# Instance norm on one core: the 32 stores move from ScalarE's queue to GpSimd's, with one packet for each DMA engine

## The chip, the cores and the metric

The kernel runs on one core of a Trainium2 chip. The core has five engines with their own instruction streams (TensorE or PE, VectorE or DVE, ScalarE or ACT, GpSimd or POOL, SyncE or SP) and 16 DMA engines that move data between HBM, the chip's main memory, and the on-chip memory (SBUF, 128 partitions). A DMA is issued by one of SP, ACT and POOL, each of which has a queue of its own on all 16 DMA engines.

The metric is the device time in microseconds (us), lower is better: 627.08 us for the kernel before, the median of 3 runs from 626.85 to 627.26. Beside it stands one profiled execution, whose trace gives the times of single instructions and DMA packets.

## The reference

Each channel of `x` (4 batches, 8 groups, 16 channels: 512 channels of 256 x 256 float32) is normalised by its own mean and variance and multiplied by its gamma. 134.2 MB go in and 134.2 MB come out.

```python
def reference(x, gamma):          # x: (4, 8, 16, 256, 256), gamma: (8, 16)
    mu = x.mean(axis=(3, 4), keepdims=True)
    var = ((x - mu) ** 2).mean(axis=(3, 4), keepdims=True)
    x_norm = (x - mu) / np.sqrt(var + 1e-5)
    out = x_norm * gamma[None, :, :, None, None]
    return out.astype(np.float32)
```

## The kernel before

The data is cut into 32 units (`U`), each of 16 channels. A channel is spread over 8 partitions (`S`), so that a unit is a tile of 128 partitions x 8192 float32 (32 KB in each partition, 4.19 MB in all). Six such tiles (`slots`, `AHEAD` = 6) lie in SBUF and are used in rotation: unit u lives in slot u mod 6, is normalised in place and stored from there. A slot can be loaded anew once its store has landed.

The order of each engine's instructions is that of the program text (`manual_schedule`); the semaphores between engines and for the DMAs are put in by the framework.

Start (L53 to L94): DVE clears a small tile `touch`, which GpSimd stores over a part of the output that is later overwritten (L54); GpSimd loads gamma into one row, `g_row` (L55). Then the first six loads are issued (L56 and L57, through `load` at L47 and L48): units 1 and 3 by ScalarE, units 0, 2, 4 and 5 by SP. DVE has 60 no-operations (L59 and L60). GpSimd builds the averaging matrix `navg` (L67 to L72), which holds -1/HW where row and column belong to the same channel. DVE copies `g_row` into `g_rep` (L83), TensorE spreads it over the partitions (L88), DVE copies the result into `g_col` (L94).

Then for each unit u (L105 to L136):

- L107, DVE: sum of each partition's row, into `st`
- L108, ACT: sum of the squares of the same row, into `st`
- L116, PE: `navg` times `st`, which gives minus the mean and minus the mean square of each channel, on all of its partitions
- L117, DVE: minus the variance; L121, ACT: its root; L125 and L127, DVE: reciprocal, times gamma
- L130, DVE: (x - mean) times scale over the whole tile, in place
- L134, ACT: the store of the tile, which waits for L130
- L136, SP: the load of unit u + 6 into the same slot, which waits until this store has landed

The next unit's Square (L108) stands behind this unit's store in ScalarE's stream. SP has nothing but loads in its stream, and GpSimd nothing at all after the start.

Of the kernel before, what the change touches and what calls it, by code (L numbers as in the profile page):

```python
# [1 line left out]

# [4 lines left out]

F32 = mybir.dt.float32
U8 = mybir.dt.uint8
ALU = mybir.AluOpType  # L10
ACTF = mybir.ActivationFunctionType
AX = mybir.AxisListType


@with_exitstack
def kernel(
    ctx: ExitStack,
    tc: tile.TileContext,
    x: bass.AP,
    gamma: bass.AP,  # L20
    out: bass.AP,
):
    nc = tc.nc
    B, G, C, H, W = x.shape
    P = nc.NUM_PARTITIONS
    HW = H * W
    n_ch = B * G * C
    S = 8
    K = P // S
    F = HW // S  # L30
    U = n_ch // K
    NG = (G * C) // K
    AHEAD = 6
    assert HW % S == 0 and (G * C) % K == 0

    xv = x.rearrange("b g c h w -> (b g c h w)").rearrange("(u p f) -> u p f", p=P, f=F)
    ov = out.rearrange("b g c h w -> (b g c h w)").rearrange("(u p f) -> u p f", p=P, f=F)
    gv = gamma.rearrange("g c -> (g c)")

    data = ctx.enter_context(tc.tile_pool(name="data", bufs=1))  # L40
    singles = ctx.enter_context(tc.tile_pool(name="singles", bufs=1))
    psum = ctx.enter_context(tc.tile_pool(name="psum", bufs=4, space=bass.MemoryType.PSUM))
    ctx.enter_context(tc.manual_schedule())

    slots = [data.tile([P, F], F32, name=f"xt{i}") for i in range(AHEAD)]

    def load(u, queue):  # L47
        queue.dma_start(out=slots[u % AHEAD][:], in_=xv[u])  # L48


    g_row = singles.tile([1, G * C], F32, name="g_row")
    touch = singles.tile([16, 128], F32, name="touch")
    nc.vector.memset(touch[:], 0.0)  # L53
    nc.gpsimd.dma_start(out=ov[0][0::S, 0:128], in_=touch[:])  # L54
    nc.gpsimd.dma_start(out=g_row[:], in_=gv[None, :])  # L55
    for u in range(AHEAD):  # L56
        load(u, nc.scalar if u in (1, 3) else nc.sync)  # L57

    for _ in range(60):  # L59
        nc.vector.nop()  # L60

    eps_t = singles.tile([P, 1], F32, name="eps_t")
    nc.gpsimd.memset(eps_t[:], 1e-5)
    one = singles.tile([1, 1], F32, name="one")
    nc.gpsimd.memset(one[:], 1.0)
    navg = singles.tile([P, K, S], F32, name="navg")
    nc.gpsimd.memset(navg[:], -1.0 / HW)  # L67
    nc.gpsimd.affine_select(  # L68
        out=navg[:], in_=navg[:], pattern=[[-S, K], [0, S]], compare_op=ALU.is_ge,
        fill=0.0, base=0, channel_multiplier=1,  # L70
    )
    nc.gpsimd.affine_select(  # L72
        out=navg[:], in_=navg[:], pattern=[[S, K], [0, S]], compare_op=ALU.is_ge,
        fill=0.0, base=S - 1, channel_multiplier=-1,
    )
    navg_w = navg[:].rearrange("p k s -> p (k s)")
    root_eps = singles.tile([P, 1], F32, name="root_eps")
    nc.scalar.activation(out=root_eps[:], in_=eps_t[:], func=ACTF.Sqrt)  # L78
    g_rep = singles.tile([1, NG, K, S], F32, name="g_rep")
    g_ps = psum.tile([P, NG], F32, name="g_ps", bufs=1)  # L80
    g_col = singles.tile([P, NG], F32, name="g_col")

    nc.vector.tensor_copy(  # L83
        out=g_rep[:],
        in_=g_row[:].rearrange("o (n k) -> o n k", n=NG).unsqueeze(3).to_broadcast([1, NG, K, S]),
    )
    for n in range(NG):
        nc.tensor.matmul(  # L88
            out=g_ps[:, n : n + 1],
            lhsT=g_rep[:, n].rearrange("o k s -> o (k s)"),  # L90
            rhs=one[:],
            start=True, stop=True,
        )
    nc.vector.tensor_copy(out=g_col[:], in_=g_ps[:])  # L94

    junk = singles.tile([P, F], U8, name="junk")

    st = singles.tile([P, U, 2], F32, name="st")
    nvar = singles.tile([P, U], F32, name="nvar")
    std = singles.tile([P, U], F32, name="std")  # L100
    rstd = singles.tile([P, U], F32, name="rstd")
    scale = singles.tile([P, U], F32, name="scale")

    squares = []
    for u in range(U):  # L105
        t = slots[u % AHEAD]
        nc.vector.reduce_sum(out=st[:, u, 0:1], in_=t[:], axis=AX.X)  # L107
        square = nc.scalar.activation(  # L108
            out=junk[:], in_=t[:], func=ACTF.Square, accum_out=st[:, u, 1:2],
        )  # L110
        if u:

            tc.declare_no_dep(square.ins, squares[-1].ins, reason="junk, ordered by the root between")
        squares.append(square)
        ps = psum.tile([P, 2], F32, name="ps")
        nc.tensor.matmul(out=ps[:], lhsT=navg_w, rhs=st[:, u], start=True, stop=True)  # L116
        nc.vector.tensor_scalar(  # L117
            out=nvar[:, u : u + 1], in0=ps[:, 0:1], scalar1=ps[:, 0:1],
            scalar2=ps[:, 1:2], op0=ALU.mult, op1=ALU.add,
        )  # L120
        nc.scalar.activation(  # L121
            out=std[:, u : u + 1], in_=nvar[:, u : u + 1], func=ACTF.Sqrt,
            bias=eps_t[:], scale=-1.0,
        )
        nc.vector.reciprocal(out=rstd[:, u : u + 1], in_=std[:, u : u + 1])  # L125
        g = u % NG
        nc.vector.tensor_mul(  # L127
            out=scale[:, u : u + 1], in0=rstd[:, u : u + 1], in1=g_col[:, g : g + 1],
        )
        nc.vector.tensor_scalar(  # L130
            out=t[:], in0=t[:], scalar1=ps[:, 0:1], scalar2=scale[:, u : u + 1],
            op0=ALU.add, op1=ALU.mult,
        )
        nc.scalar.dma_start(out=ov[u], in_=t[:])  # L134
        if u + AHEAD < U:
            load(u + AHEAD, nc.sync)  # L136


# [1 line left out]
_INS = ['x', 'gamma']  # L140
_OUTS = [((4, 8, 16, 256, 256), 'float32')]


# [23 lines left out]
```

## Time and profile before

| | |
|---|---|
| median of 3 runs | 627.08 us (626.85 to 627.26) |
| span of the profiled execution | 625.8 us |
| moved by DMA | 268.46 MB, mean 429 GB/s over the span |
| DVE busy | 443.4 us (71%) |
| ACT busy | 238.8 us (38%) |
| PE busy | 21.4 us (3%) |
| POOL busy | 2.4 us |
| L107, reduce, DVE | 32 x 8684 ns |
| L130, scale, DVE | 32 x 4550 ns |
| L108, square, ACT | 32 x 7030 ns |
| load 31 has landed, L107 of unit 31 starts | at 586.12 us |
| store 31 is issued | at 601.17 us |

The span goes from the first to the last instruction of the program in the profiled execution; the runs' time is that of the whole execution on the device. Busy times of different engines overlap. A DMA's issue is a short instruction on the engine that issues it; the transfer runs by itself afterwards, and the profile gives its time to landing, from the issue until the completion semaphore. Queue numbers stand for the issuer: 1 is SP's, 10 is ScalarE's, 0 is GpSimd's.

### The profile page before, as it was taken

How to read it: one execution, taken by the hardware profiler on the slowest of the kernel's cores; microseconds unless marked ns; L12 is line 12 of the kernel's file. 1: busy time of each engine (PE TensorE's matmuls, PEld its weight loads, DVE VectorE, ACT ScalarE, POOL GpSimd, SP SyncE). 2: the span in 40 equal slices, each digit the busy share in tenths (PEclk: the TensorE clock that was granted, in tenths of full speed). 3: DMA queues.
4: the chain of work that ended last, by engine and by line, in shares of the span. 5: the costliest groups of instructions: out<-in, count | busy, mean ns of one | idle time of the engine just before them, and what ended most of it. 6: DMA issues, size and time to landing. Idle time of an engine off the chain costs nothing.

```text
span 625.8 us, 631 instructions
## 1 busy us (share of the span) xinstructions
PE 21.4 (3%) x80; PEld 19.5 (3%) x80; DVE 443.4 (71%) x163; ACT 238.8 (38%) x98; POOL 2.4 (0%) x11
## 2 busy tenths in 40 slices
PE   0200000000000000000000000000000000000000
PEld 0200000000000000000000000000000000000000
DVE  0588999999776687766776667867668676686730
ACT  0444444444443244432344423444224442244400
POOL 1000000000000000000000000000000000000000
DMA  8999999999999999999999999999999999999998
GB/s 369 436 415 429 429 436 436 436 436 434 424 434 434 434 436 434 431 429 434 436 436 436 436 431 427 431 436 431 436 434 434 429 434 436 436 436 436 429 425 354
DMA packets 9282, 268.46 MB, mean 429 GB/s; under 512 B 1072, under 2 KB 1088, under 8 KB 1088
## 3 DMA queue, kind: packets, MB, share of 16 engines
q10 hardware_dynamic: 4896, 142.61, 52.9%
q1 hardware_dynamic: 4320, 125.83, 46.7%
q0 software_dynamic: 64, 0.01, 0.0%
q14 instruction: 2, 0.02, 0.0%
HBM read 134.22 MB, written 134.23 MB: 429 GB/s over the span
## 4 chain that ended last, share of the span: by engine, by line
another core or an unknown queue 61%; DMA 17%; DVE 15%; SPq 1%; PE 1%; issue 0%; ACT 0%
DVE st L107 10%; DMA xt<-in_x_dram 10%; DMA out_dram<-xt 8%; DVE xt L130 5%; SPq L48 1%; PE ps L116 1%; ACT std L121 0%; DVE nvar L117 0%; DVE rstd L125 0%; DVE scale L127 0%
## 5 line engine op out<-in xcount | busy, mean ns | idle before, releaser
L107 DVE TENSOR_REDUCE st<-xt 128x1 f32<-128x8192 f32 x32 | 277.9, 8684 | 101.2 <-DMA xt<-in_x_dram 101.2
L108 ACT ACTIVATE junk<-xt 128x8192 uint8<-128x8192 f32 x32 | 225.0, 7030 | 276.0 <-DMA xt<-in_x_dram 232.8
L130 DVE TENSOR_SCALAR xt<-xt,ps,scale 128x8192 f32<-128x8192 f32 x32 | 145.6, 4550 | 1.2
L121 ACT ACTIVATE std<-nvar,eps_t 128x1 f32<-128x1 f32 x32 | 9.4, 294 | 79.6 <-DVE nvar L117 79.6
L116 PE MATMUL ps<-st,navg 128*128 128x2 f32 x64 | 17.9, 349 | 558.0 <-DVE st L107 558.0
L116 PEld LDWEIGHTS ps<-st,navg 128*128 128x128 f32 x64 | 16.0, 311 | 559.8 <-issue 559.8
L117 DVE TENSOR_SCALAR nvar<-ps 128x1 f32<-128x1 f32 x32 | 9.2, 287 | 23.8 <-PE ps L116 23.8
L125 DVE RECIPROCAL rstd<-std 128x1 f32<-128x1 f32 x32 | 5.2, 164 | 11.6 <-ACT std L121 11.6
L83 DVE COPY g_rep<-g_row 1x1024 f32<-1x1024 f32 x1 | 0.7, 680 | 14.3 <-DMA g_row<-in_gamma_dram 14.3
L108 ACT ACTIVATION_READ_ACCUMULATOR junk<-xt 128x1 f32 x32 | 6.0, 187 | 0.0
L127 DVE TENSOR_TENSOR scale<-rstd,g_col 128x1 f32<-128x1 f32 x32 | 5.1, 159 | 1.1
L88 PE MATMUL g_ps<-one,g_rep 1*128 1x1 f32 x16 | 3.5, 346 | 16.2 <-DVE g_rep L83 16.2
L88 PEld LDWEIGHTS g_ps<-one,g_rep 1*128 1x128 f32 x16 | 3.5, 325 | 16.1 <-issue 16.1
L94 DVE COPY g_col<-g_ps 128x8 f32<-128x8 f32 x1 | 0.2, 166 | 3.7 <-PE g_ps L88 3.7
L78 ACT ACT_TABLE_LOAD x1 | 1.3, 1283 | 1.7 <-PEq L151 1.7
L53 DVE MEMSET touch<- 16x128 f32 x1 | 0.2, 165 | 0.9 <-PEq L151 0.9
L54 POOL DMA_DIRECT2D out_dram<-touch x1 | 0.6, 619 | 0.8 <-DVE touch L53 0.8
L55 POOL DMA_DIRECT2D g_row<-in_gamma_dram x1 | 0.5, 487 | 0.0
L68 POOL TENSOR_SCALAR_AFFINE_SELECT navg<-navg 128x128 f32<-128x128 f32 x1 | 0.4, 400 | 0.1
L72 POOL TENSOR_SCALAR_AFFINE_SELECT navg<-navg 128x128 f32<-128x128 f32 x1 | 0.4, 399 | 0.1
L67 POOL MEMSET navg<- 128x128 f32 x1 | 0.2, 232 | 0.0
L78 ACT ACTIVATE root_eps<-eps_t 128x1 f32<-128x1 f32 x1 | 0.2, 202 | 0.0
(6 smaller groups left out, 0.6 us busy)
## 6 DMA issues: line engine op xcount, KB each, us to landing
out_dram<-xt ACTq DMA_DIRECT2D x32, 4096.0 KB, 62.5
xt<-in_x_dram SPq DMA_DIRECT2D x30, 4096.0 KB, 38.5
xt<-in_x_dram ACTq DMA_DIRECT2D x2, 4096.0 KB, 31.6
out_dram<-touch POOLq DMA_DIRECT2D x1, 8.0 KB, 9.1
g_row<-in_gamma_dram POOLq DMA_DIRECT2D x1, 0.5 KB, 13.3
```

Source lines behind the costliest of these rows:

```text
L48: queue.dma_start(out=slots[u % AHEAD][:], in_=xv[u])
L78: nc.scalar.activation(out=root_eps[:], in_=eps_t[:], func=ACTF.Sqrt)
L83: nc.vector.tensor_copy(out=g_rep[:], in_=g_row[:].rearrange("o (n k) -> o n k", n=NG).unsqueeze(3).to_broadcast([1, NG, K, S]),)
L88: nc.tensor.matmul(out=g_ps[:, n : n + 1], lhsT=g_rep[:, n].rearrange("o k s -> o (k s)"), rhs=one[:], start=True, stop=True,)
L107: nc.vector.reduce_sum(out=st[:, u, 0:1], in_=t[:], axis=AX.X)
L108: square = nc.scalar.activation(out=junk[:], in_=t[:], func=ACTF.Square, accum_out=st[:, u, 1:2],)
L116: nc.tensor.matmul(out=ps[:], lhsT=navg_w, rhs=st[:, u], start=True, stop=True)
L117: nc.vector.tensor_scalar(out=nvar[:, u : u + 1], in0=ps[:, 0:1], scalar1=ps[:, 0:1], scalar2=ps[:, 1:2], op0=ALU.mult, op1=ALU.add,)
L121: nc.scalar.activation(out=std[:, u : u + 1], in_=nvar[:, u : u + 1], func=ACTF.Sqrt, bias=eps_t[:], scale=-1.0,)
L125: nc.vector.reciprocal(out=rstd[:, u : u + 1], in_=std[:, u : u + 1])
L127: nc.vector.tensor_mul(out=scale[:, u : u + 1], in0=rstd[:, u : u + 1], in1=g_col[:, g : g + 1],)
L130: nc.vector.tensor_scalar(out=t[:], in0=t[:], scalar1=ps[:, 0:1], scalar2=scale[:, u : u + 1], op0=ALU.add, op1=ALU.mult,)
```

## The change

The 32 stores are issued by GpSimd instead of ScalarE, with `single_packet=True`, which asks for all descriptors (single contiguous pieces of a transfer) that one DMA engine gets from this DMA to be put in one packet. The 60 no-operations of DVE are taken out. ScalarE keeps the loads of units 1 and 3, SP the others. The order of all other instructions on each engine stays; as three lines are gone, what was L130 before is L127 after, and the store is L131.

```diff
     for u in range(AHEAD):
         load(u, nc.scalar if u in (1, 3) else nc.sync)
-
-    for _ in range(60):
-        nc.vector.nop()

     eps_t = singles.tile([P, 1], F32, name="eps_t")
...
             out=t[:], in0=t[:], scalar1=ps[:, 0:1], scalar2=scale[:, u : u + 1],
             op0=ALU.add, op1=ALU.mult,
         )
-        nc.scalar.dma_start(out=ov[u], in_=t[:])
+        nc.gpsimd.dma_start(out=ov[u], in_=t[:], single_packet=True)
         if u + AHEAD < U:
             load(u + AHEAD, nc.sync)
```

## The prediction, made before the changed kernel was run

> **What bounds the kernel now.** I read the page's slices first, then its queues, then the waits of the SP queue, then the end of the timeline. The slices (40 equal stretches of the span) and the queues:
>
> ```profile
> DVE  0588999999776687766776667867668676686730
> ACT  0444444444443244432344423444224442244400
> POOL 1000000000000000000000000000000000000000
> DMA  8999999999999999999999999999999999999998
> ...
> q10 hardware_dynamic: 4896, 142.61, 52.9%
> q1 hardware_dynamic: 4320, 125.83, 46.7%
> ```
>
> See the DMA row: 9 from the second slice to the last but one, while VectorE (DVE) leaves gaps. 268.46 MB at the plateau of 433 GB/s take 620 us of the 625.8 us span, so the DMA engines bound the kernel, and a change is worth what it makes them idle or stops them idling. Queue 10 is ScalarE's (32 stores and two loads, 34 x 4.19 MB), queue 1 is SP's (30 loads). 4896 packets over 34 transfers are 144 each: 128 rows of 32 KB and 16 small ones, so 8 rows for each of 16 engines.
>
> The packet records give the order on one DMA engine. Late in the run, while both queues hold work, it takes one 32,768-byte packet of queue 1, one of queue 10, and so on, 1.209 us from start to start. A transfer alone is thus 8 x 1.209 = 9.68 us, and a store and a load together 19.36. At the start GpSimd's queue shows its turns too: the 512-byte row of `touch` at 7.34 us, between a row of queue 10 and one of queue 1, and its own 4-byte completion packet only a full round of the three queues later, at 9.79. One turn is one row, on all three queues, as things are.
>
> The waits of the SP queue, and the end of the timeline (start, duration, what):
>
> ```profile
> SPq L48 <- DMA out_dram<-xt: 535.3, 26, 59.6
> SPq L162 <- DMA out_dram<-xt: 38.4, 4, 9.6
> SPq L162 <- DMA xt<-in_x_dram: 38.2, 1, 38.2
> ```
>
> ```profile
> 586.12 8.69 DVE L107 TENSOR_REDUCE st<-xt 128x1 f32<-128x8192 f32 x1 [4.33 <-DMA xt<-in_x_dram]
> ...
> 596.59 4.55 DVE L130 TENSOR_SCALAR xt<-xt,ps,scale 128x8192 f32<-128x8192 f32 x1
> 601.17 0.34 ACTq L134 DMA_DIRECT2D out_dram<-xt  x1
> ```
>
> SP waits 26 times for a store to free a slot. At the end (L162) it waits for the last load and then for four store landings of 9.6 us each: when load 31 lands at 586.1, three older stores are still queued, 29 us of transfer. The compute of unit 31 (586.12 to 601.17, 15.05 us) lies wholly under that backlog. This cover is what the change may take away.
>
> ```profile
> out_dram<-xt ACTq DMA_DIRECT2D x32, 4096.0 KB, 62.5
> xt<-in_x_dram SPq DMA_DIRECT2D x30, 4096.0 KB, 38.5
> ```
>
> A store takes 62.5 us to land, three turns' worth of 19.36 behind its elders; a load takes two. 62.5 + 38.5 + 15.05 = 116 = 6 slots x 19.36: the slots are all in use and most sit in the store queue.
>
> **The change, part by part.**
>
> *The 60 no-operations on DVE go.* No instruction of theirs stands in the trace, and they lie between the `touch` memset (0.89 us) and the copy at L83 (15.33 us), for which DVE idles 14.27 us, waiting for g_row. Cost 0; without that cover, 60 sequencer steps of 0.02 us (the "issue" pieces of the chain) would be 1.2 us.
>
> *ScalarE loses 32 issues of 0.34 us and the wait in front of them.* Its next Square (L108) no longer stands behind the scale (L130); that wait was 43.2 us of its idle time in all. But reduce (8.69 us) starts with Square (7.03) at the earliest and ends later, on DVE, after the same L130. Gain 0: DVE's 15.05 a unit hides it.
>
> *GpSimd gets 32 issues.* Nothing else is on it after 3.7 us, so nothing is queued behind them but the next store, and that needs a later L130 anyway. Each waits for DVE as before, and also for the store eight issues earlier on its semaphore, which the slot rotation of six has already required. Issue rows there are 0.62 us (16 rows) and 0.49. From end of issue to first packet: at least 1.0 (SP's first load, 0.81 to 1.80, on an empty queue), at most 5.4 (`touch`, 1.98 to 7.34, of which some is queueing behind rows of 1.2 us). I take 2.0, nearer to the empty queue, because the price will matter only where the DMA is empty.
>
> The Trainium skill ("SBUF — State Buffer", Who interferes with whom) says that descriptors of a GpSimd DMA cannot be written while VectorE runs a two-port operation; L130, at 4.55 us against 8.69 for the reduce over the same elements, looks like one. A store is issued when its own L130 ends, and the next is 10.5 us away, so by that rule too the sum stays.
>
> *All descriptors of an engine in one packet.* If a turn is a packet, a store now holds the engine for 8 rows, 9.68 us, and then lets one load row pass. Total work is the same 620 us and the load queue keeps it fed, so nothing changes in mid-run. What changes is who waits. A store lands in some 9.68 + 1.2 to 2.4 + 2 = about 14 us instead of 62.5; the slots it gives back go to the load queue, where loads then stand 116 - 15 - 14 = 87 us instead of 38.5. Stores no longer pile up, so at the end nothing older is left to run while units 30 and 31 are computed.
>
> Walk the last units, from the landing of load 29 at T, with DVE free. Loads alone land load 30 at T+9.7. Store 29 is ready at T+15.05+2 = T+17; until then load 31 gets 6 rows, then the store runs to T+26.7, then the 2 rows left: load 31 lands at T+29.1. DVE works without a break to T+30.1 (unit 30) and T+45.15 (unit 31). Store 30 starts at T+32.1: the DMA has been idle 3.0. It ends at T+41.8; store 31 starts at T+47.2: idle 5.4. Sum 8.4 us of idle DMA that the old backlog filled. Bounds: at best store 30 follows the last load at once, and only the 15.05 - 9.68 = 5.4 is left; at worst store 30 is done when load 31 lands, and 15.05 + 2 = 17 stand open (20.4 with 5.4 of latency).
>
> Sum: 625.8 (the profiled span) + 8.4 = 634.2. The runs' median of 627.08 lies 1.3 over the span (what stands around the first and last instruction), so **635.5 us**. Its own range is 5.4 to 14 us of idle, 632.5 to 641.
>
> **The rivals.**
>
> *A turn stays one row, whatever the packet (not slower).* For it: every switch in the records is after one row. Against: on both hardware queues and for `touch` each row may be a packet by itself, so these rows can't tell a packet from a row, and the flag alters just that. Store and load would alternate as now, three stores would be left at 586 us, and the latency on GpSimd would vanish in a queue of 62.5 us: 625.8 + 1.3 = 627.1. This is also the case in which the flag does nothing. The point that decides is the backlog: with 15 us of stores or more at the last load's landing, nothing is lost.
>
> The Trainium skill ("DMA: Bandwidth & Descriptors", Issuing engines are not separate DMA queues) says that DMAs of all issuers share the 16 engines and interleave, which alone would leave the time at this value. The same page (Queues, rings and completion order) lets an engine drain a whole packet before it switches, which is the forecast's mechanism; no run here shows it for a packet of more than one row.
>
> *Turns change and the issue on GpSimd is slow.* 128 rows are 8 times `touch`'s 16: if its 0.62 us grows in proportion, 5 us, and the 5.4 to the first packet holds, store 31 starts 10.4 instead of 2 us after its L130. Against: the two issues present, of 16 rows and of one row in 16 parts, can't separate a fixed cost from one by rows. Mid-run the load queue hides it; at the end it adds 8.4: 643.9.
>
> *Faster.* Longer packets could save something between rows, and the first store's switch of queues. Bound: the best slices run at 436 GB/s; 268.46 MB at that are 615.7 us, and with 1.8 us to the first packet and 1.3 after the last one 618.8, 7 under the span. But 1.209 us a row is 433.5 GB/s already, so half of the rows in longer packets would give 2 us, 625, and only if the backlog stays.
>
> **How the numbers follow.** Forecast 0.70, one row a turn 0.12, slow issue 0.12, faster 0.06. A change under 0.2% (1.25 us) can't be told from none here. Faster takes the last rival, 0.06; same takes the second case less a little, 0.11; slower the rest, 0.83. The range goes from 626.7, which takes in the case of equal turns, to 642, which leaves out most of the slow issue: about 0.84 inside.
>
> **What would show it.** Right: the stores' time to landing falls to 10 to 20 us and the loads' rises to 80 or more; the SP queue's last wait for a load is followed by one or two store landings instead of four; the DMA row drops below 9 in the last two slices, with a gap of about 5 us before the last store, and stays at 9 elsewhere. Wrong: stores still at some 60 us (equal turns); POOL issue rows of several us, or a gap from L130 to the first store packet beyond 5 us (slow issue); a DMA row with holes in mid-run, which would mean that the load queue runs dry and my cover is not there.

## The result, and the profile after

The changed kernel takes 630.04 us (median of 8 runs, 628.11 to 632.29) against 627.14 us (median of 8, 626.79 to 627.58): ratio 1.0046, 95% interval 1.0033 to 1.0060. It is slower by 2.9 us; 8.4 were forecast. The eight runs lie in two groups, with nothing between: 628.1 to 629.1 (four runs, spans 626.1 to 627.1) and 631.0 to 632.3 (four runs, spans 629.0 to 630.3). The profiled execution is of the lower group.

First the page of the kernel after: slices of the DMA engines, queues, and times to landing.

```profile
DMA  8999999999999999999999999999999999999997
GB/s 368 435 416 431 433 428 433 435 435 435 433 435 435 435 428 431 433 431 435 435 435 433 435 433 435 431 433 428 435 435 435 435 435 435 435 435 433 426 431 318
...
q0 software_dynamic: 4672, 134.23, 49.6%
q1 hardware_dynamic: 4320, 125.83, 46.6%
q10 hardware_dynamic: 288, 8.39, 3.2%
...
out_dram<-xt POOLq DMA_DIRECT2D x32, 4096.0 KB, 62.2
xt<-in_x_dram SPq DMA_DIRECT2D x30, 4096.0 KB, 38.5
xt<-in_x_dram ACTq DMA_DIRECT2D x2, 4096.0 KB, 31.7
```

The stores are on queue 0 now, GpSimd's, but they still take 62.2 us to land and the loads 38.5: both queues go on sharing the engines row by row. 4672 packets are 32 x 144 and 64 of `touch` and gamma, so the flag did not even merge the records. The DMA row has no hole.

The end of the timeline (start, duration, what), the end of the chain of waits, and SP's last waits in the same kernel; the last line is SP's wait for the other engines at the close in the kernel before:

```profile
596.59 4.55 DVE L127 TENSOR_SCALAR xt<-xt,ps,scale 128x8192 f32<-128x8192 f32 x1
601.44 0.53 POOL L131 DMA_DIRECT2D out_dram<-xt  x1 [18.84 <-DVE xt L127]
```

```profile
562.71 0.53 POOL out_dram L131
563.24 18.82 issue
582.05 0.02 POOLq L131
582.07 0.53 POOL out_dram L131
582.60 18.82 issue
601.42 0.55 POOLq L159
```

```profile
SPq L159 <- DMA out_dram<-xt: 76.6, 3, 47.9
SPq L159 <- PEq L159: 1.8, 2, 1.3
...
SPq L162 <- PEq L162: 0.7, 2, 0.5
```

L127 ends at 601.14, as L130 did before, so compute and loads are where they were. The last chain, which ended in DVE before, now ends in GpSimd's sequencer, at the closing instructions (L159 stands for the end of the program). And SP, which before waited 0.5 us at most for the other engines at the close (0.7 in two waits), waits 1.3. The last DMA packet of x ends at 624.48 us after and at 624.49 before: in this execution nothing was lost until then.

The trace's instruction table shows what closes the program. GpSimd's DRAIN at L159 ends at 626.25 us, 1.77 us after its last store's last packet and 1.07 after SP has finished (625.18); before, it had ended at 15.43 us, 0.44 after gamma's load, and only SP's end (624.97) counted. What follows takes 0.85 us after and 0.83 before. So the lower group has an explanation to be tested, a closing drain of 1.1 us, and the upper group, another 3 us, has none yet.

### The profile page after: what moved, and what is told of

Its sections match the earlier page's. It is cut to its first block, busy times and chain, and to the rows that moved or that the text cites. A ratio compares the mean times of both kernels' runs of the same rounds, so it can differ in the third digit from the quotient of the medians.

```text
span 627.1 us, 631 instructions
## 1 busy us (share of the span) xinstructions
PE 21.4 (3%) x80; PEld 19.5 (3%) x80; DVE 443.3 (71%) x163; ACT 238.1 (38%) x98; POOL 19.5 (3%) x43
## 3 DMA queue, kind: packets, MB, share of 16 engines
q0 software_dynamic: 4672, 134.23, 49.6%
## 4 chain that ended last, share of the span: by engine, by line
another core or an unknown queue 48%; DMA 17%; DVE 15%; issue 13%; SPq 1%; PE 1%; ACT 0%; POOL 0%; POOLq 0%
DVE st L104 10%; DMA xt<-in_x_dram 10%; DMA out_dram<-xt 8%; DVE xt L127 5%; SPq L48 1%; PE ps L113 1%; ACT std L118 0%; DVE nvar L114 0%; POOL out_dram L131 0%; DVE rstd L122 0%; DVE scale L124 0%; POOLq L159 0%; POOLq L131 0%
## 5 line engine op out<-in xcount | busy, mean ns | idle before, releaser
L127 DVE TENSOR_SCALAR xt<-xt,ps,scale 128x8192 f32<-128x8192 f32 x32 | 145.6, 4550 | 1.2
L131 POOL DMA_DIRECT2D out_dram<-xt x32 | 17.0, 533 | 581.2 <-DVE xt L127 581.2
L80 DVE COPY g_rep<-g_row 1x1024 f32<-1x1024 f32 x1 | 0.7, 680 | 14.4 <-DMA g_row<-in_gamma_dram 14.4
## 6 DMA issues: line engine op xcount, KB each, us to landing
out_dram<-xt POOLq DMA_DIRECT2D x32, 4096.0 KB, 62.2
xt<-in_x_dram SPq DMA_DIRECT2D x30, 4096.0 KB, 38.5
```

The costliest lines, as they stand in the source:

```text
L127: nc.vector.tensor_scalar(out=t[:], in0=t[:], scalar1=ps[:, 0:1], scalar2=scale[:, u : u + 1], op0=ALU.add, op1=ALU.mult,)
L131: nc.gpsimd.dma_start(out=ov[u], in_=t[:], single_packet=True)
```

## The experiments

### The flag, and what a turn is

**Flag off.**

```diff
-        nc.gpsimd.dma_start(out=ov[u], in_=t[:], single_packet=True)
+        nc.gpsimd.dma_start(out=ov[u], in_=t[:])
```

> The changed kernel with the one-packet flag taken off the 32 stores; all else as changed. Theory A (a turn is one 32 KB row whatever the flag says, and the 2.9 us come from GpSimd's own queue): the flag is inert, same time as the changed kernel, ratio to before 1.003 to 1.006, stores land in 62 us. Theory B (the flag itself costs the time, for instance by longer turns somewhere): back to 627.1, ratio 0.999 to 1.001.

Measured: 628.77 us (11 runs, 628.26 to 632.19), ratio 1.0038, interval 1.0025 to 1.0051, again in two groups (seven runs at 628.3 to 628.8, four at 630.4 to 632.2). Theory A: without the flag the kernel is the changed kernel. Its profiled execution (span 628.4) is of the upper group and is used below.

**Turns of small stores with and without the flag.**

```diff
-    AHEAD = 6
+    AHEAD = 5
...
     nc.gpsimd.dma_start(out=g_row[:], in_=gv[None, :])
+    wide = singles.tile([P, 4096], F32, name="wide")
+    nc.vector.memset(wide[:], 0.0)
+    nc.gpsimd.dma_start(out=ov[20][:, 0:128], in_=wide[:, 0:128], single_packet=True)
+    nc.gpsimd.dma_start(out=ov[21][:, 0:1024], in_=wide[:, 0:1024], single_packet=True)
+    nc.gpsimd.dma_start(out=ov[22][:, 0:4096], in_=wide[:], single_packet=True)
+    nc.gpsimd.dma_start(out=ov[23][:, 0:128], in_=wide[:, 0:128])
```

> The kernel before with five slots and, early on, four further small stores by GpSimd behind g_row, of 128 rows each (8 for each DMA engine): 512 B rows, 4 KB rows and 16 KB rows with the one-packet flag, and 512 B rows without. Its output is the reference's, since these places are stored over later; its time is not compared. The packet records show the turns. Theory A1 (a turn is one descriptor whatever the flag): each of the 8 rows and the completion takes a turn of its own, one every 2.4 us while two other queues are busy, for all four. Theory A2 (a flagged packet is taken whole): the flagged ones come as 9 records on end with no other queue between, the unflagged one row by row. Theory A3 (whole only up to a size): whole for 512 B, row by row at 16 KB.

Packet records of one DMA engine: start in us, queue, bytes. Queue 0 has the small stores; queues 1 and 10 have rows of x.

```
16.85 q0  4096   512 B rows, flag: 8 rows in one record
17.00 q1 32768
18.21 q10 32768
19.42 q0     4   its completion, a turn later
...
21.90 q0  4096   4 KB rows, flag: one row
22.06 q0  4096   one row (the other two queues had just completions here)
22.22 q1 32768
23.43 q10 32768
24.64 q0  4096   one row
...
43.32 q0 16384   16 KB rows, flag: one row
43.94 q0 16384   one row
44.55 q1 32768
45.76 q10 32768
46.97 q0 16384   one row
...
69.95 q0  4096   512 B rows, no flag: 8 rows in one record
70.11 q0     4   its completion
```

(One run, 638.85 us, which is not compared, since this kernel has a slot less.) Eight 512 B rows go in one turn, as one record of 4096 bytes, with the flag and without. Rows of 4 KB and of 16 KB take a turn each in spite of the flag, and so does the completion. In this trace a turn holds 4 KB of small rows or one longer row; a row of x has 32 KB. Theory A3 had the flagged stores right, the small rows whole and the 16 KB rows one by one; none of the three had the small rows without the flag go together as well. So the size of a row decides here and the flag does not; rows of 4 KB and 16 KB were not tried without it.

### The closing drain

**Store 31 alone on GpSimd.**

```diff
-        nc.scalar.dma_start(out=ov[u], in_=t[:])
+        if u == U - 1:
+            nc.gpsimd.dma_start(out=ov[u], in_=t[:], single_packet=True)
+        else:
+            nc.scalar.dma_start(out=ov[u], in_=t[:])
```

> The kernel before, but store 31 alone is issued by GpSimd with the flag; 31 stores stay on ScalarE, the 60 no-operations stay. Theory A (the closing drain of GpSimd): one software DMA at the very end is enough, 629 to 631 as in the changed kernel. Theory B (a cost for each store): 627.1 to 627.3. As store 31 is alone on its queue it should finish before store 30, about 4 to 5 us before the end, so the drain may be partly hidden: then between the two, 627.1 to 629.

Measured: 627.38 us (11 runs, 627.22 to 628.10), ratio 1.0009, interval 1.0000 to 1.0017. The store did not finish early: its last packet is at 624.47. But the drain ended 0.67 us after it, at 625.13, before SP was done (625.40). Neither theory's number: the time lies where a partly hidden drain was expected, but for another reason than the one given there. One software DMA at the end is not enough to be seen, since the drain after it is short. Over all traces the drain tends to be longer the more software DMAs there were since the start, though their number alone does not give it. From the last software DMA's completion to the drain's end it is 0.43 and 0.44 us after 2 of them, 0.67 after 3, 0.57 after 4, 1.00 after 6, 1.12 and 1.45 after 18, 1.68 to 1.89 after 31, 1.86 after 33, 1.75 to 1.77 after 34, and 1.98 after 36.

**The last three stores on ScalarE.**

```diff
+        if u < U - 3:
             nc.gpsimd.dma_start(out=ov[u], in_=t[:], single_packet=True)
+        else:
+            nc.scalar.dma_start(out=ov[u], in_=t[:])
```

> The changed kernel, but the stores of units 29, 30 and 31 issued by ScalarE; GpSimd issues the other 29 with the flag. By the one-row turns of the DMA engines its last store then lands about 8 us before the end. Theory A (GpSimd's closing DRAIN, which ended 1.1 us after SP's last wait in the changed kernel, is what is added, because it can only end after GpSimd's last software DMA): the drain is over before the last store lands, span 625.8, time 627.1 to 627.9. Theory B (each store costs a little more on GpSimd's queue, spread over the run): 29 of 32 stores keep the cost, 629.6 to 630.0.

Measured: 632.58 us (4 runs, 632.30 to 633.36), ratio 1.0090, interval 1.0077 to 1.0103. Slower than both theories had it, for a reason of its own. Its windows over the close (stretch, its length, busy time of each engine, clock, DMA share, GB/s):

```profile
547.00:600.00 53.00, 1.11 (x4) 1.00 (x4) 27.26 (x10) 14.39 (x6) 0.00 (x0) 1.00 1.01 418
600.00:615.10 15.10, 0.56 (x2) 0.50 (x2) 13.85 (x5) 7.42 (x3) 0.00 (x0) 1.00 0.91 395
615.10:630.30 15.20, 0.00 (x0) 0.00 (x0) 0.00 (x0) 0.00 (x0) 0.00 (x0) 1.00 0.72 308
```

With two queues of stores beside the one of loads, the loads got one turn in three: load 31 landed at 600.0 us instead of 586.1, and by the time unit 31 was computed (615.1) too little of the older stores was left. The DMA share falls to 0.72, and in the packet records each of the 16 engines is idle for 3.3 us on average between 610 us and the last row's end, against 1.1 in the kernel before. The drain did end early (620.91), but the run can't tell the theories apart. It fits the step of the prediction that the change itself never reached, that a backlog taken away at the end costs microseconds. It does not show that step alone: the third queue also put the engines out of step, with the 16 completions of load 31 lying 5.3 us apart, and the two effects were not separated.

**The first or the last sixteen stores on GpSimd.**

```diff
+        if u < U // 2:       # the other kernel: u >= U // 2
             nc.gpsimd.dma_start(out=ov[u], in_=t[:], single_packet=True)
+        else:
+            nc.scalar.dma_start(out=ov[u], in_=t[:])
```

> The changed kernel, but the stores of units 16 to 31 issued by ScalarE; GpSimd issues the first 16 only. The change of queue lies in mid-run, where the DMA engines have other work; at the end the backlog of three stores is as before, so nothing is uncovered. Theory A (GpSimd's closing drain, some 1.75 us after its last software DMA in the changed kernel, plus 0.25 us outside the span): the drain ends about 390 us, span 625.0 to 625.8, time 626.9 to 627.4, in all runs alike. Theory B (rows fetched through GpSimd's queue now and then hold up one DMA engine, so that the slowest of 16 ends later; half of the changed kernel's runs came out 3 us above the other half): 16 of 32 stores keep half of that, 627.5 to 629 with the two groups of runs still to be seen.

> The counterpart: units 0 to 15 stored by ScalarE, 16 to 31 by GpSimd with the flag. Theory A: the drain is at the end again, 628 to 628.5 in the lower group of runs; if the drain grows with the number of software DMAs it is between 0.6 (one store) and 1.75 us (32 stores) after the last landing. Theory B: 16 of 32 stores keep half of the mid-run loss, as in the first-half kernel, on top of that.

Measured: 649.23 us (6 runs, 644.72 to 651.99), ratio 1.0347 (1.0319 to 1.0374), and 668.24 us (6 runs, 661.48 to 670.27), ratio 1.0647 (1.0609 to 1.0686). Far outside what any theory expected, and no test of the drain. From the change of queue in mid-run on, the 16 DMA engines no longer finish together: the 16 completions of a store or load lay 1.2 us apart before it, and those of loads grew to 20 us apart after it in the first kernel and to 38 in the second. A load counts as landed when the slowest engine has it. This made the engines' step the thing to look at.

**The last three stores on SP,** which has issued its last load by then, so that no third queue comes in.

```diff
+        if u < U - 3:
             nc.gpsimd.dma_start(out=ov[u], in_=t[:], single_packet=True)
+        else:
+            nc.sync.dma_start(out=ov[u], in_=t[:])
```

> The changed kernel, but the stores of units 29, 30 and 31 issued by SP, whose queue runs empty there; no third queue comes in, and GpSimd's last store lands some 19 us before the end, so its closing drain is over in time. Theory A for the lower group (the drain, some 1.2 us at the end): lower group at spans 625.0 to 625.8 and times 626.9 to 627.8, and the upper group of Theory C 2 to 3 us above it. If the drain is not what is lost: lower group at 626.1 and more, 628.1 and more.

Measured: two groups, six runs at 627.21 to 627.47 (spans 625.5 to 625.8) and five at 629.13 to 631.54; median 627.47, ratio 1.0026, interval 1.0011 to 1.0041. SP's waits, and its times to landing:

```profile
SPq L134 <- DVE xt L127: 52.3, 3, 18.9
SPq L162 <- DMA out_dram<-xt: 23.1, 3, 9.6
SPq L151 <- PEq L151: 0.8, 1, 0.8
SPq L162 <- PEq L162: 0.7, 2, 0.5
```

```profile
out_dram<-xt POOLq DMA_DIRECT2D x29, 4096.0 KB, 62.3
out_dram<-xt SPq DMA_DIRECT2D x3, 4096.0 KB, 33.3
```

SP's wait for the other engines at the close is back at 0.5 us: GpSimd's drain ended at 606.48. The lower group is at the level of the kernel before, and what lies outside the span is back too: 1.7 us, as before, against 2.0 in the changed kernel. So the closing drain is most of the lower group's loss: between the means of the two lower groups (628.55 and 627.36) lie 1.2 us, some 0.3 of them outside the span. The 0.2 us that are left to the kernel before stay open. The upper group is untouched by the edit.

### The upper group: engines out of step

**The changed kernel twice more,** for its trace.

> The changed kernel once more, for its trace. Its eight runs fell in two groups, spans 626.1 to 627.1 and 629.0 to 630.3, and the first profile (627.1) is of the lower one. If this one is of the upper group, Theory B wants the last store's landing late on few DMA engines (a spread of more than 2 us between the 16 completions, 1.5 in the first profile) with the middle engine as before; a longer closing drain instead would show as more than 1.75 us between the last landing and the drain's end.

> The changed kernel a third time, for its trace, with the same two readings: spread of the 16 completions against length of the closing drain.

Measured: spans 630.5 (632.49 us, upper group) and 626.7 (628.65 us, lower). The drain is 1.76 us in both. The last store's completions lie 4.93 us apart in the upper execution and 1.22 in the lower, as Theory B had it, and the difference begins in the rows. The sequence of one DMA engine from store 0 on (L a row of a load, S of a store, small letters their completions), first as on 14 engines of the upper execution, then as on the two others. The records carry no engine number; an engine is followed by its rows, which lie end to end in time.

```
LSLSLSLSLSLSLSLSlsLSLSLSLSLSLSLSLSlsLSLS
LLSLSLSLSLSLSLSlSLsLSLSLSLSLSLSLSlSLsLSL
```

On these two engines store 0 missed its first turn (LL), and from then on each load is done there one row before its store. In the lower execution all 16 engines begin alike. In the upper profile of the flag-off kernel one engine has the second pattern. The GB/s of the upper execution (40 slices), and the landings:

```profile
GB/s 366 432 428 432 430 432 434 432 432 429 432 432 430 432 432 433 432 432 432 432 432 432 432 432 432 432 430 434 430 434 432 441 434 431 432 432 432 432 432 235
...
out_dram<-xt POOLq DMA_DIRECT2D x32, 4096.0 KB, 64.7
xt<-in_x_dram SPq DMA_DIRECT2D x30, 4096.0 KB, 36.5
```

The plateau is 432 instead of the 435 of the first profile, and the last slice is half empty (235): most engines are done and the late ones still write. Stores land 2.5 us later and loads 2 us earlier, as the two engines' order says. The table sums up the profiles of the kernels that have the early loads where the kernel before has them and all stores on one queue:

| kernel | spread of the 16 completions of store 0 | of the last store | largest of a load | span |
|---|---|---|---|---|
| before | 0.43 us | 1.64 | 1.64 | 625.8 |
| changed | 0.49 | 1.54 | 1.60 | 627.1 |
| changed again | 0.37 | 1.22 | 1.22 | 626.7 |
| changed again, upper | 2.38 | 4.93 | 3.72 | 630.5 |
| flag off, upper | 2.06 | 3.02 | 1.81 | 628.4 |

A late start of 2 us on one or two engines stays and grows over 560 us: in each upper profile, one or two completions of every store lie over 1 us behind the others. No run of the kernel before took over 627.7 us. There store 0 stands behind load 3 in ScalarE's own queue and takes its turns over, on each engine at the same place. On GpSimd's queue it starts by itself, close to the moment when load 3 ends (its last row ends between 41.2 and 41.7 us on the 16 engines of the upper execution), and an engine either catches the turn or not: its first row starts at 43.1 to 43.4 us on 14 engines and at 45.3 and 45.6 on the other two.

**The early loads moved.** Three edits of one line (L57) and combinations of them.

```diff
     for u in range(AHEAD):
-        load(u, nc.scalar if u in (1, 3) else nc.sync)
+        load(u, nc.sync)                                  # all on SP
...
+        load(u, nc.gpsimd if u in (1, 3) else nc.sync)    # two on GpSimd
```

The changed kernel with all early loads on SP, and the same with the last three stores on SP:

> The changed kernel with the loads of units 1 and 3 on SP too, so that ScalarE's queue is empty and only two queues hold rows when store 0 starts. Theory C (in the changed kernel three queues hold rows when store 0 starts at 38 us, ScalarE's last load among them, which in some runs puts a DMA engine out of step with the others for good; its stores land 3 us late at the end): the upper group of runs is gone, spans 626.0 to 627.0, all runs 628.0 to 628.9, spread of the 16 completions of the last store under 2 us. Theory D (rows from GpSimd's queue delay an engine at any time): still two groups, spans up to 630. The closing drain stays in both.

> Both edits: the six first loads on SP, the last three stores on SP, the other 29 on GpSimd with the flag. Theories A and C together account for all of the 2.9 us but some 0.25 us outside the span: one group, spans 625.0 to 625.8, time 626.9 to 627.5, ratio to before 0.999 to 1.001. If something else is lost on GpSimd's queue, over 628.

The kernel before with two early loads on GpSimd:

> The kernel before with the loads of units 1 and 3 on GpSimd instead of ScalarE: the stores stay on ScalarE, no software DMA is near the end, but three queues hold rows when store 0 starts. Theory C: two groups of runs, spans 625 to 626 and 628 to 630. Theory D: one group, spans 625.0 to 625.8, times 626.7 to 627.6.

Measured: 643.54 us (6 runs, 632.69 to 646.23), 644.71 us (6 runs, 634.04 to 645.34), and 627.67 us (11 runs, 627.39 to 628.12; ratio 1.0009, 1.0001 to 1.0018). Theory C fell on both sides. With two queues only, even the lowest runs of the first two (632.69 and 634.04) lie above every run of the changed kernel; with three queues at the start, the third has one group, though a few tenths above Theory D's 627.6. In the first two, store 0 starts in the middle of a load: the spread of its completions is 1.6 and 1.8 us, and that of the loads grows to 7.5 and 15.5 us. In the third, eight engines begin store 0 at 34.6 to 35.1 us and eight at 37.6 to 38.0, but its completions lie only 0.68 us apart: these engines were level again when store 0 was done. So a late first row by itself does not cost the time.

This left the question whether GpSimd's queue has a part in it. **The kernel before with all early loads on SP:**

> The kernel before with all six first loads on SP; the stores stay on ScalarE, so no software DMA moves any rows of x. Store 0 now has ScalarE's queue to itself and starts in the middle of a load. Theory E (stores and loads that are out of step on the DMA engines make engines fall behind, whatever queue issues them): as slow as the changed kernel with the loads on SP, 632 to 646, spread of the completions growing to several us. Theory D (rows of GpSimd's queue are what delays an engine): 626.7 to 627.6 as before.

Measured: 644.14 us (4 runs, 641.82 to 644.51), ratio 1.0266, interval 1.0249 to 1.0282. GpSimd moves no row of x here. The GB/s of the kernel before, then this kernel's slices and landings:

```profile
GB/s 369 436 415 429 429 436 436 436 436 434 424 434 434 434 436 434 431 429 434 436 436 436 436 431 427 431 436 431 436 434 434 429 434 436 436 436 436 429 425 354
...
DMA  9999999999999999999999999999999999999986
GB/s 370 447 394 445 424 422 430 426 434 404 437 416 424 430 417 428 412 434 432 408 430 416 432 424 414 428 420 426 426 408 424 422 424 432 412 422 418 430 367 296
...
xt<-in_x_dram SPq DMA_DIRECT2D x32, 4096.0 KB, 56.6
out_dram<-xt ACTq DMA_DIRECT2D x32, 4096.0 KB, 48.1
```

The median slice has 424 GB/s where 434 were, with the DMA engines at 9 up to the last two slices: the rows themselves take longer. A row of a load takes 1264 ns on average (up to 2722) against 1218 (up to 2087) in the kernel before. An engine has 256 such rows, so this alone is some 12 of the 17 us. Store 0's completions are 2.7 us apart, those of loads 12 us at the end. Theory D, that GpSimd's rows are the cause, has fallen.

**The changed kernel with store 0 behind load 3 on GpSimd's queue,** and the same with the last three stores on SP:

> The changed kernel with the loads of units 1 and 3 on GpSimd, so that store 0 stands behind load 3 in the same queue, as in the kernel before. Theory E: store 0 can't miss a turn, no upper group, all spans 626.1 to 627.0, times 628.0 to 629.0 (the closing drain stays), spread of the last completions under 2 us. Theory D: upper group as in the changed kernel, up to 632.

> The same, and the stores of units 29, 30 and 31 issued by SP, so that GpSimd's closing drain ends some 18 us before the last landing. Both causes taken away: one group, spans 625.0 to 625.8, times 626.9 to 627.5, ratio to before 0.999 to 1.001. Over 628 in any run would mean that something else is lost.

Measured: 628.87 us (6 runs, 628.75 to 628.94), ratio 1.0030 (1.0018 to 1.0041), and 627.64 us (11 runs, 627.53 to 628.05), ratio 1.0010 (1.0001 to 1.0019). One group in each; the upper group is gone, and the second edit takes off 1.2 us more. The page of the first:

```profile
GB/s 369 435 435 401 435 435 435 435 435 435 433 435 435 435 433 435 429 431 431 431 433 435 431 431 435 435 435 435 435 435 433 433 435 435 435 433 431 431 433 318
...
out_dram<-xt POOLq DMA_DIRECT2D x32, 4096.0 KB, 76.5
xt<-in_x_dram SPq DMA_DIRECT2D x30, 4096.0 KB, 24.2
```

The plateau is 435 again, the last store's completions are 1.06 us apart. The expectation of the second (626.9 to 627.5) was missed by a few tenths; the kernel before with the same two loads on GpSimd, 627.67, is 0.5 us above its own against 0.7 here, so most of that comes with the early loads there and not with the stores.

One thing was not as Theory E put it. In the first of these two kernels the stores' completions stand 4.8 us before the loads' in the packet records, so the two kinds are four rows out of step with each other, at no cost. What the slow profiles have in common is that the engines differ among themselves. Leaving out the kernel with five slots, the completions of store 0 are 1.6 to 2.7 us apart in five slow profiles (spans of 628.4 to 642.8 us). In the eight profiles with spans of 625.6 to 627.1 us they are 0.7 apart at most. The three kernels whose queue of stores changes to or from ScalarE in mid-run or for the last three stores begin level and differ from the change on. That is an order of events and not a mechanism: why a row then takes longer was not tried.

## Why the prediction was right or wrong

**The step that failed** is "If a turn is a packet, a store now holds the engine for 8 rows". A turn stayed one row, flag or not: the stores land in 62.2 us, and the small stores of 4 KB and 16 KB rows keep to single rows. The backlog therefore stayed: after load 31 (586.1 us) four more stores landed, at 595.8, 605.5, 615.1 and 624.8 us, as before. The 8.4 us of idle DMA never came to pass; between 610 us and the last row the engines are idle for 1.0 us on average, against 1.1 before. None of the marks named for it is seen in the profile: no gap before the last store, and loads at 38.5 us instead of 80. The prediction said that the records could not tell a packet from a row and then gave the flag the benefit of it, at 0.70; the rival with turns of one row had 0.12 and was right.

The Trainium skill ("DMA: Bandwidth & Descriptors", SWDGE vs HWDGE vs iDMA) gives a packet as at most 4096 bytes by preference and as the boundary at which an engine changes queues. The 4096-byte records of eight 512 B rows agree with that, and a row of 32 KB, far beyond it, was one turn. The prediction leaned on the same page's sentence about draining whole packets and did not ask how large one gets.

**The rival's own time** of 627.1 was wrong too, since it had no term for the close. GpSimd's drain was seen nowhere in the sum; the trace of before had it, 0.44 us after gamma's load landed, where it cost nothing. Taking it away gave 1.2 us, some 0.3 of them outside the span. The second missing term is the step of the DMA engines: 0 in half of the runs and about 3 us in the other half. The median of 630.04 stands between two groups and is the time of neither. That it lies inside the stated range of 626.7 to 642, and that the kernel came out slower at all, was luck: both costs that made it so are missing from the sum, and the forecast's own 632.5 to 641 holds no run.

**Two smaller readings were off** and changed nothing. The 1.3 us around the span compares a median with another execution's span; each run of the kernel before lies some 1.7 us over its own span (627.49 and 625.8 in one). The least time from end of issue to first packet was counted from the issue's start: SP's first load is issued from 0.81 to 1.17 us and its first packet starts at 1.80, so it is 0.6 and not 1.0.

**What held.** Faster was hardly possible with the DMA engines at 9 throughout, and wasn't. DVE's no-operations were hidden: L80 still waits for gamma, 14.4 us idle before it against 14.3. ScalarE's freed queue gained nothing. The issue on GpSimd costs 0.53 us for 128 rows, less than the 0.62 for `touch`'s 16, so the rival of a slow issue had no ground. The worth of the backlog may be right in kind: with the last three stores on ScalarE it was partly taken away, and 3.3 us of idle DMA stood at the end instead of 1.1, though there the engines were out of step as well.

**Point by point of what would show it:** time to landing, no (62.2 us, the sign named for equal turns); one or two landings after SP's last load, no (L127 of unit 31 ends at the same time as before and the last packets end at 624.48); DMA row below 9 in the last two slices, no (only the last one, as before); no holes in mid-run, yes.

## What to carry to other kernels

When two queues share the DMA engines all the time, ask whether the DMA engines are still level when the first transfer of each queue is done. Here a store queue that began behind a load in its own queue ran at 435 GB/s. One that began alone in mid-load beside a single load queue lost 17 us when ScalarE issued it and 5.5 us or more when GpSimd did; beside two other queues, the same start cost nothing in one kernel and 3 us in half of the runs of another. A queue moved to GpSimd brings a drain to the end of the program that must be counted, or covered by giving the last transfers to another queue that is already in use. Where a time falls in two groups, take a profile of each before explaining a median.

## What the runs showed of the hardware that was not expected

- A turn of a DMA engine held one row from 4 KB up, or eight rows of 512 B as one record of 4096 bytes; the completion took a turn of its own. The one-packet flag changed nothing for rows of 512 B and 32 KB, and did not join rows of 4 KB and 16 KB.
- GpSimd's closing DRAIN ended 0.44 us after its last software DMA when there had been 2 of them, and 1.68 to 1.98 us after it with 31 to 36.
- One engine that missed one turn at 43 us was still late at the end, some 580 us on. A kernel that moved the same bytes over the same two hardware queues, with its engines out of step, took 644 us instead of 627, its load rows stretching from 1218 to 1264 ns on average. What stretches them is open.
- A change of the store queue in mid-run cost 22 and 41 us.
